# Weight chunks held behind the first row fetch, one branch moved, and stores and fetches of the expert stage reordered

## The chip, the cores and the metric

One of the eight cores of a Trainium2 chip runs the kernel. The metric is the device time of one execution in microseconds (us); the number given for the kernel before is the median of three runs. The profile is one further execution, and all positions in it are us from the start of its span.

## What is computed

The reference is one decoder layer on 576 tokens (512 of a prompt, 8 times 8 of samples) with a model width of 1024: a mixer of gated linear attention and dilated attention, a cross attention, a hierarchical mixture of experts, and a final normalisation. The change concerns the last two. Cut to what matters, that is:

```python
def hier_moe(x, w_gr, b_gr, w_er, b_er, w_e1, w_e3, w_e2):   # x: (576, 1024), normalised
    g_idx = jnp.argmax(x @ w_gr + b_gr, axis=-1)             # 4 groups, one for each token
    sel = (x @ w_er + b_er).reshape(N, 4, 8)[group g_idx]    # 8 experts in a group
    top_l, top_i = lax.top_k(sel, 2)                         # two experts for each token
    gate = p_group * softmax(top_l)
    y[token] = sum over its two experts e of
        gate * ((silu(x @ w_e1[e]) * (x @ w_e3[e])) @ w_e2[e])
h = h + hier_moe(rmsnorm(h, g3), ...)
y = rmsnorm(h, g_final)
```

Each of the 32 experts has 6 MB of float32 weights (two matrices of 1024 x 512 and one of 512 x 1024), so 192 MB are read whatever the tokens choose. Before this stage the kernel computes the mixer and the cross attention (some 580 us); the change does not touch them, apart from two memsets and from the weight loads that begin beside their end.

## The kernel before

**Tokens.** A route block computes group, experts and gates, and sorts the tokens: those of a group stand in 256 places, two tiles of 128 places each, tiles 2g and 2g+1. `pay` holds for each place the token's number (0 in an empty place) and its gates. The finished rows of the hidden state are written to a buffer in DRAM, `rows_d`, six 256 KB or smaller writes on GpSimd's queue and the last two on ScalarE's (L1111, L1120). GpSimd fetches a tile with an indirect DMA (`fetch_rows`, L1060) whose index `src` holds one row for each place, row 0 for an empty one. The first two tiles are fetched at the end of the route block (`i_first` is the second fetch), tiles 2 and 3 in the first pair, tiles 4 and 5 in pair 5 and tiles 6 and 7 in pair 9 (`fetch_group`, L1339), each into one of the four tiles `acc[:, t % 4]`. The same `acc` then collects the experts' output, so a tile can be fetched only after the finished rows of the tile that held its place before are stored.

**Pairs.** The loop at L1555 runs over 16 pairs of experts, p = 0 to 15; group g has pairs 4g to 4g+3. For each pair `slots_of` (L1476) builds four one-hot matrices `oh` on VectorE, `gather` (L1484) multiplies the group's rows with them on TensorE (32 matmuls at L1492) and brings the result into `X` (L1498 on ScalarE, L1500 on VectorE). The rows are split into two parts of float32 first, `pthi` on ScalarE and `ptlo` on VectorE (`split_group`, L1468, by lines L243 and L244), once for a group. Then come 64 matmuls with the weights w13 (L1566), the gated activation (L1588, L1591), four transposes (L1594), 32 matmuls with w2 (L1607), and `combine` (L1519), which adds the weighted result to `acc`. `scales` (L1502) prepares the weights of the places (L1510, L1513). The gather for the next pair is issued within the current one. After the last pair of a group `finish` (L1365) normalises its two tiles and stores them with two indirect DMAs on GpSimd's queue (`store_rows`, L1361); for the last group `last_norm` (L1534 to L1550) does this.

**Weights.** The 192 MB come as 12 chunks of 1 MB for each pair (8 of w13, 4 of w2; the last pair's w2 as 8 halves) into a ring of 18 buffers, issued by SyncE's queue (SP) in order (L1312, L1320, L1327), at most 8 in flight. A buffer is free again when the matmuls that read it are done. A manual dependency makes the chunk that is the sixteenth of the ring wait until `i_first` has landed:

```python
            if len(ring) == CHUNK_A + 3:
                tc.add_manual_dep(i_w.ins, i_first.ins.name, ..., reason="the first rows before more weights")
```

**Branch.** `general` (L1438) is a branch of the program that handles rare distributions of tokens; here it is not taken, and costs each engine the branch itself. It stands in pair p = GENERAL.

**Order.** A scheduler sets each engine's instruction order from the order of the code and the dependencies it finds; all engines then run their lists in order, with waits on semaphores between them. The names of lines in the rows are those of the kernel before.

Of the kernel before, what the change touches and what calls it, by code (L numbers as in the profile page):

```python
# [26 lines left out]
EPS = 1e-6  # L27
CHUNK_A, CHUNK_B = 13, 5
PAY = 24
GENERAL = 11  # L30
CUT = 128
KV = 4
OC = 2
# [142 lines left out]
def body(ctx: ExitStack, tc: tile.TileContext, I, O, dbg=None):  # L176
# [879 lines left out]
        ve.tensor_scalar(f[:, 0:1], id_, -1.0, 0.0, op0=OP.add, op1=OP.max)  # L1056
        ve.tensor_copy(out, f[:, 0:1])

    def fetch_rows(out, index):
        return gp.indirect_dma_start(out=out, out_offset=None, in_=rows_d[:, :],  # L1060
                                     in_offset=bass.IndirectOffsetOnAxis(ap=index, axis=0))

    def place_hot(out, at):

# [8 lines left out]
    def payload(ts, hots, bank):  # L1073

        for t, hot in zip(ts, hots):
            by_place(bank[:, (t - ts[0]) * 3 * PAY:(t - ts[0] + 1) * 3 * PAY], hot, pay3)
        n = len(ts) * PAY
        x = bank[:, 0:3 * n].rearrange("p (t s c) -> p t c s", s=3, c=PAY)
        ve.tensor_reduce(pay[:, ts[0]:ts[0] + len(ts)], x, axis=AX.X, op=OP.add)
        for t in ts:  # L1080
            row_index(dst[:, t:t + 1], pay[:, t], False)

    with ExitStack() as st:
        rp = pool(st, "route")
        space = acc.rearrange("p a c -> p (a c)")
        acc3, last = space[:, 0:T], space[:, T:2 * T]
        stage = [space[:, 2048 + i * 512:2560 + i * 512].rearrange("p (i c) -> p i c", c=128) for i in range(3)]
        stage4 = space[0:64, 3584:4096]
        hots = [space[:, a:a + 320].bitcast(BF16).rearrange("p (i c) -> p i c", c=128) for a in (2048, 3072)]
# [217 lines left out]
    def load_one(p, n):  # L1307

        w = wchunk()
        if n < 8:  # L1310
            q, h = divmod(n, 2)
            i_w = sy.dma_start(w, I["w13"][2 * p + h, q])  # L1312
            if len(ring) == CHUNK_A + 3:
                tc.add_manual_dep(i_w.ins, i_first.ins.name, mybir.DependencyInfo(
                    mybir.DependencyClass.Sync, mybir.DependencyReason.DATA), reason="the first rows before more weights")
            w = w.rearrange("p (k c) -> p k c", k=2)
            views[p, "in", q, h] = lambda k2, c: w[:, k2, c * 512:c * 512 + 512]
        elif p < 15:
            c, h = divmod(n - 8, 2)
            sy.dma_start(w, I["w2"][2 * p + h, c])  # L1320
            w = w.rearrange("p (j c) -> p j c", j=4)
            views[p, "out", c, h] = lambda j: w[:, j]
        else:
            c = n - 8
            w = w.rearrange("p (h j c) -> p h j c", h=2, j=4)
            for h in range(2):
                sy.dma_start(w[:, h], I["w2"][2 * p + h, c // 2].rearrange("p (j c) -> p j c", j=4)[  # L1327
                    :, :, c % 2 * 256:c % 2 * 256 + 256])
            views[p, "out", c, 0] = lambda j: w[:, 0, j]
            views[p, "out", c, 1] = lambda j: w[:, 1, j]  # L1330
# [8 lines left out]
    def fetch_group(g):  # L1339
        ts = [2 * g, 2 * g + 1]  # L1340
        for t in ts:
            read_index(src[:, t:t + 1], pay[:, t, 20:21])
            fetch_rows(acc[:, t % 4], src[:, t:t + 1])

    def payload_late(ts):
        bank = cp_()
        for i, t in enumerate(ts):
            hot = hot_()
            place_hot(hot, at8[:, :, t:t + 1])
            by_place(bank[:, i * 3 * PAY:(i + 1) * 3 * PAY], hot, pay3)  # L1350
        n = len(ts)
        ve.tensor_reduce(pay[:, ts[0]:ts[0] + n], bank[:, 0:3 * n * PAY].rearrange("p (t s c) -> p t c s", s=3, c=PAY),
                         axis=AX.X, op=OP.add)
        for t in ts:
            row_index(dst[:, t:t + 1], pay[:, t], False)

    loads_to(RING)
    gf = mw.tile([128, D], F32, name="gf")
    gp.dma_start(gf, I["g_fin"].to_broadcast([128, D]))

    def store_rows(x, index):  # L1361
        gp.indirect_dma_start(out=O["y"][:, :], out_offset=bass.IndirectOffsetOnAxis(ap=index, axis=0), in_=x, in_offset=None,
                              bounds_check=T - 1, oob_is_err=False)

    def finish(tiles):  # L1365

        n = len(tiles)
        s = mw.tile([128, 2, 2], F32, name="ss")
# [7 lines left out]
        ac.activation(r, r, AF.Exp, scale=-0.5)  # L1376
        for i, (a, index) in enumerate(tiles):
            ve.scalar_tensor_tensor(a, a, r[:, i:i + 1], gf, op0=OP.mult, op1=OP.mult)
            store_rows(a, index)


    def features(rows_, Xe):
# [151 lines left out]
    def last_norm(c, cs):  # L1534
# [8 lines left out]
        else:  # L1543
# [3 lines left out]
            gp.tensor_scalar(a[:, 0:CUT], a[:, 0:CUT], r, None, op0=OP.mult)  # L1547
            ac.activation(a[:, CUT:512], a[:, CUT:512], AF.Copy, scale=r)
            ve.scalar_tensor_tensor(a[:, 512:], a[:, 512:], r, gf[:, 512:D], op0=OP.mult, op1=OP.mult)
            store_rows(a, dst[:, 6 + c:7 + c])  # L1550

    split_group(0)
    oh, X = slots_of(0), tokens_x()
    so, done, nxt = None, None, None
    for p in range(16):  # L1555
        if p == 0:
            gather(0, oh, X, range(4))
        if p % 2 == 0 and p < 14 and p != GENERAL - 1:
            nxt = slots_of(p // 2 + 1), tokens_x()
        so = scales(p, oh)  # L1560
        H = [hp_(), hp_()]
# [7 lines left out]
        with tc.issue_after(i_h.ins):  # L1569
# [6 lines left out]
                payload_late([4, 5, 6, 7])  # L1576
            if p % 4 == 1 and 4 < p < 12:
                fetch_group(p // 4 + 1)
            if p % 4 == 2 and p < 14:
                split_group(p // 4 + 1)  # L1580
            if p == GENERAL:
                general()
                nxt = slots_of(p // 2 + 1), tokens_x()
                gather(p // 2 + 1, *nxt, range(4))
            elif nxt:
                gather(p // 2 + 1, *nxt, range(2) if p % 2 == 0 else range(2, 4))
        sg = mw.tile([128, 512], F32, name="sg")
        ac.activation(sg, H[0], AF.Silu, scale=sv[:, 0:1])  # L1588
        if p == 15:
# [23 lines left out]
                        combine(y, oT, p, z, last_norm)  # L1613
        if p % 4 == 0 and p:
            g = p // 4 - 1
            finish([(acc[:, t % 4], dst[:, t:t + 1]) for t in (2 * g, 2 * g + 1)])
        done = y, oT, p
        if p % 2 and nxt:
            (oh, X), nxt = nxt, None
# [15 lines left out]
```

## Time and profile before

| what | us |
|---|---|
| median of the three runs | 1088.97 |
| lowest and highest of them | 1088.72, 1091.85 |
| the profiled execution, its own time | 1092.6 |
| its span in the profile | 1090.9 |
| TensorE (PE) busy in the span | 1011.1 (93%) |
| VectorE (DVE), ScalarE (ACT), GpSimd (POOL) busy | 454.9, 342.2, 61.5 |
| mean granted TensorE clock, full speed is 1 | 0.961 |

The page gives, for 40 slices of the span, the busy share of each engine, the granted TensorE clock and what the DMA engines moved. The expert stage fills the slices from the 23rd on, where the DMA engines move 400 to 422 GB/s until the last slice; in the slices before, the rate lies between 29 and 350 GB/s. The clock is at 0.7 in four slices and at 0.8 to 0.9 or more in the others. A wait row names the waiting engine and line, then what ended the wait, then the total, the count and the longest wait, all in us.

### The profile page before, as it was taken

To read this page: it belongs to the slowest core of one execution; us is meant where nothing else is said; L and a number is where in the kernel's file an instruction comes from. 1 tells how busy PE (TensorE), PEld (TensorE's weight loads), DVE (VectorE), ACT (ScalarE), POOL (GpSimd) and SP (SyncE) were. 2 spreads that over 40 slices of the span, in tenths; PEclk is the share of its full clock that TensorE was granted. 3 is DMA by queue.
4 is the path that set the end of the run, shared out by engine and by line. 5 is a ranking of instruction groups with operands and counts; after the bars stand their busy time and mean duration, and the time that the engine had idled before them with its cause. 6 is when DMAs were issued, how large, how long until landed. Compare 5 with 4: busy or idle time off the path is not lost. (4 is left out here: it accounts for less than half of the span.)

```text
span 1090.9 us, 17977 instructions
## 1 busy us (share of the span) xinstructions
PE 1011.1 (93%) x7375; PEld 717.2 (66%) x7375; DVE 454.9 (42%) x1031; ACT 342.2 (31%) x696; POOL 61.5 (6%) x85
## 2 busy tenths in 40 slices
PE   8999999999999999999995699999599959799995
PEld 7998889886769999888995344445244434254432
DVE  6337775357555754554335224223222322113213
ACT  5355323367443533333322112113111311024103
POOL 2100011000000200000111000001000010001002
PEclk9999999999999999999997799999799979999998
DMA  7312115526785743564785499999999999999992
GB/s 254 118 39 78 29 57 232 208 72 225 313 314 175 263 172 123 204 209 180 271 350 198 176 417 422 420 421 422 421 421 420 421 420 422 419 420 421 420 402 100
DMA packets 59674, 301.91 MB, mean 277 GB/s; under 512 B 6935, under 2 KB 13576, under 8 KB 35136
## 3 DMA queue, kind: packets, MB, share of 16 engines
q1 hardware_dynamic: 53856, 282.66, 66.4%
q0 software_dynamic: 5120, 17.73, 4.4%
q8 instruction: 59, 0.97, 0.4%
q10 hardware_dynamic: 608, 0.30, 0.1%
q14 instruction: 31, 0.25, 0.1%
HBM read 290.30 MB, written 12.19 MB: 277 GB/s over the span
## 5 line engine op out<-in xcount | busy, mean ns | idle before, releaser
L1566 PE MATMUL hp<-wc,X 128*64 128x512 f32 x1024 | 229.4, 593 | 1.2 <-DMA wc<-w 1.2
L1566 PEld LDWEIGHTS hp<-wc,X 128*64 128x64 f32 x1024 | 89.1, 137 | 135.8 <-issue 127.5
L283 PE MATMUL pj<-hi,whi 128*128 128x288 f32 (+1 forms) x544 | 163.3, 301 | 0.9 <-ACT R1t L193 0.5
L283 PE MATMUL pj<-hi,wlo 128*128 128x288 f32 (+1 forms) x544 | 162.8, 299 | 0.0
L283 PE MATMUL pj<-lo,whi 128*128 128x288 f32 (+1 forms) x544 | 162.3, 299 | 0.0
L1607 PE MATMUL hp<-wc,sg 128*64 128x512 f32 (+1 forms) x544 | 121.4, 586 | 0.1
L234 ACT ACTIVATE whi<-wst 128x1024 fp32r<-128x1024 f32 (+1 forms) x62 | 65.6, 1058 | 148.0 <-PE pj L283 120.8
L283 PEld LDWEIGHTS pj<-hi,whi 128*128 128x128 f32 x544 | 103.4, 190 | 4.8 <-issue 2.6
L283 PEld LDWEIGHTS pj<-hi,wlo 128*128 128x128 f32 x544 | 103.7, 191 | 1.7 <-issue 1.4
L283 PEld LDWEIGHTS pj<-lo,whi 128*128 128x128 f32 x544 | 103.6, 190 | 1.3 <-issue 0.8
L235 DVE TENSOR_TENSOR wlo<-wst,whi 128x1024 fp32r<-128x1024 f32 (+1 forms) x62 | 76.0, 1226 | 44.8 <-ACT whi L234 44.8
L1607 PEld LDWEIGHTS hp<-wc,sg 128*64 128x64 f32 x544 | 39.2, 140 | 70.5 <-issue 66.7
L1591 DVE SCALAR_TENSOR_TENSOR sg<-hp,sv,sg 128x512 f32<-128x512 f32 x16 | 12.0, 749 | 162.8 <-PE hp L1566 154.7
L1588 ACT ACTIVATE sg<-hp,sv 128x512 f32<-128x512 f32 x16 | 11.0, 687 | 185.3 <-PE hp L1566 185.3
L1528 DVE TENSOR_TENSOR acc<-acc,cp 128x512 f32<-128x512 f32 (+1 forms) x66 | 42.3, 666 | 62.1 <-PE cp L1526 61.7
L244 DVE TENSOR_TENSOR ylo<-hp,yhi 128x512 fp32r<-128x512 f32 (+1 forms) x34 | 22.4, 659 | 78.5 <-ACT yhi L243 78.5
L308 PE MATMUL pj<-whi,hi 128*128 128x256 f32 (+1 forms) x184 | 52.9, 288 | 0.0
L308 PE MATMUL pj<-wlo,hi 128*128 128x256 f32 (+1 forms) x184 | 52.5, 286 | 0.0
L308 PE MATMUL pj<-whi,lo 128*128 128x256 f32 (+1 forms) x184 | 52.4, 285 | 0.0
L1492 PE MATMUL xp<-oh,pthi 128*128 128x256 f32 x128 | 35.5, 308 | 16.4 <-DVE oh L1480 9.2
L243 ACT ACTIVATE yhi<-hp 128x512 fp32r<-128x512 f32 (+1 forms) x34 | 19.4, 572 | 87.0 <-PE hp L1607 87.0
L1492 PEld LDWEIGHTS xp<-oh,pthi 128*128 128x128 f32 x128 | 27.3, 213 | 17.7 <-issue 16.9
(440 smaller groups left out, 1661.0 us busy)
## 6 DMA issues: line engine op xcount, KB each, us to landing
wc<-w SPq DMA_DIRECT2D x188, 1024.0 KB, 19.8
kv<-kc SPq DMA_DIRECT2D x16, 768.0 KB, 6.9
kv<-vc SPq DMA_DIRECT2D x16, 768.0 KB, 5.2
ckv<-mkc SPq DMA_DIRECT2D x16, 512.0 KB, 6.1
ckv<-mvc SPq DMA_DIRECT2D x16, 512.0 KB, 5.8
wst<-w_qkb SPq DMA_DIRECT2D x8, 512.0 KB, 3.7
wst<-w_mk SPq DMA_DIRECT2D x8, 512.0 KB, 5.5
wst<-w_mv SPq DMA_DIRECT2D x8, 512.0 KB, 4.5
```

Of the source, the lines that this page charges most:

```text
L234: ac.activation(hi[:, s], w[:, s], AF.Copy)
L235: ve.tensor_tensor(lo[:, s], w[:, s], hi[:, s].bitcast(F32), op=OP.subtract)
L243: ins = ac.activation(hi, x, AF.Copy)
L244: ve.tensor_tensor(lo, x, hi.bitcast(F32), op=OP.subtract)
L283: pe.matmul(p, lhsT=a[:, k], rhs=b[k][:, c], start=(k == 0 and s == 0), stop=(k == KT - 1 and s == 2))
L308: pe.matmul(outs[i][0:m], lhsT=a[xk][:, i * 128:i * 128 + m], rhs=b[:, k, :], start=(kh == 0 and k == 0 and s == 0 and head), stop=(kh == ...
L1492: pe.matmul(ps[:, k * 256:k * 256 + 256], lhsT=pt[s][:, c, kk * 128:kk * 128 + 128], rhs=oh[:, c], start=(k + c + s == 0), stop=(k + c + s ...
L1528: ve.tensor_tensor(a, a, ps, op=OP.add)
L1566: i_h = pe.matmul(H[c][rows[e]], lhsT=X[:, k, at + e * 64:at + e * 64 + 64], rhs=views[p, "in", k // 2, e](k % 2, c), start=(k == 0), stop ...
L1588: ac.activation(sg, H[0], AF.Silu, scale=sv[:, 0:1])
L1591: ve.scalar_tensor_tensor(sg, H[1], sv[:, 1:2], sg, op0=OP.mult, op1=OP.mult)
L1607: i_y = pe.matmul(Y[rows[e]], lhsT=hT_[:, j, rows[e]], rhs=views[p, "out", c, e](j), start=(j == 0), stop=(j == 3))
```

## The change

1. The manual dependency holds for the last three chunks of the ring (16th to 18th), where before it held for the 16th alone.
2. `slots_of(0)` is written ahead of `split_group(0)`, and the store index `dst` of the first two tiles is computed with those of tiles 2 and 3 later, in the first pair.
3. `GENERAL` is 9, where it was 11: the branch stands in the tenth pair. `split_group` of the next group is written in the pairs with p % 4 == 3, where it was p % 4 == 2; the next pair's slots are made, and gathered, to match.
4. The stores of finished rows are declared independent of one another.
5. Tiles 2 to 7 are fetched with an index that lies outside the buffer for an empty place, and such a place is left out by the DMA. `acc` is set to 0 once beforehand (two memsets on GpSimd, while the attention runs), since an empty place keeps what was there.

```diff
-GENERAL = 11
+GENERAL = 9
...
-    def fetch_rows(out, index):
+    def fetch_rows(out, index, some=False):
+        kw = dict(bounds_check=T - 1, oob_is_err=False) if some else {}
         return gp.indirect_dma_start(out=out, out_offset=None, in_=rows_d[:, :],
-                                     in_offset=bass.IndirectOffsetOnAxis(ap=index, axis=0))
+                                     in_offset=bass.IndirectOffsetOnAxis(ap=index, axis=0), **kw)
...
         ve.tensor_reduce(pay[:, ts[0]:ts[0] + len(ts)], x, axis=AX.X, op=OP.add)
-        for t in ts:
-            row_index(dst[:, t:t + 1], pay[:, t], False)
...
+        gp.memset(space[:, 2 * T:2048], 0.0)
+        gp.memset(space[64:128, 3584:4096], 0.0)
...
-            if len(ring) == CHUNK_A + 3:
+            if CHUNK_A + 2 < len(ring) <= RING:
...
-            read_index(src[:, t:t + 1], pay[:, t, 20:21])
-            fetch_rows(acc[:, t % 4], src[:, t:t + 1])
+            row_index(src[:, t:t + 1], pay[:, t], None)
+            fetch_rows(acc[:, t % 4], src[:, t:t + 1], True)
...
-        for t in ts:
+        for t in ts if ts[0] > 2 else [0, 1] + ts:
             row_index(dst[:, t:t + 1], pay[:, t], False)
...
+        if static:
+            for b in stored:
+                tc.declare_no_dep(i.ins, b, reason="other rows")
+            stored.append(i.ins)
...
+    oh, X = slots_of(0), tokens_x()
     split_group(0)
-    oh, X = slots_of(0), tokens_x()
...
-        if p % 2 == 0 and p < 14 and p != GENERAL - 1:
+        if p % 4 == 0 and p != GENERAL - 1 or p % 4 == 3 and p < 15:
             nxt = slots_of(p // 2 + 1), tokens_x()
...
-            if p % 4 == 2 and p < 14:
+            if p % 4 == 3 and p < 15:
                 split_group(p // 4 + 1)
...
             elif nxt:
-                gather(p // 2 + 1, *nxt, range(2) if p % 2 == 0 else range(2, 4))
+                gather(p // 2 + 1, *nxt, (range(2), range(2, 4), None, range(4))[p % 4])
```

On SyncE, where the ring is first filled, the last six loads stood like this before (the brackets hold the semaphores that a load waits for: HW ones belong to DMAs of SP and ACT, SW ones to DMAs of GpSimd; DMASW0 is here the first row fetches):

```order
L1312 DMA wc_6741<-w 128x2048 [waits DMAHW2_49]
L1312 DMA wc_6743<-w 128x2048 [waits DMAHW3_49,PE_49]
L1312 DMA wc_6745<-w 128x2048 [waits DMAHW6_49,PE_49]
L1312 DMA wc_6749<-w 128x2048 [waits DMAHW7_49]
L1312 DMA wc_6751<-w 128x2048 [waits DMAHW0_49,DVE_49]
L1312 DMA wc_6747<-w 128x2048 [waits DMAHW1_49,DMASW0_49]
```

With the change the same place reads (lines after the first insertion are a line or more further on):

```order
L1313 DMA wc_6731<-w 128x2048 [waits DMAHW2_49]
L1313 DMA wc_6733<-w 128x2048 [waits DMAHW3_49,PE_49]
L1313 DMA wc_6735<-w 128x2048 [waits DMAHW6_49,PE_49]
L1313 DMA wc_6737<-w 128x2048 [waits DMAHW7_49,DMASW0_49]
L1313 DMA wc_6739<-w 128x2048 [waits DMAHW0_49]
L1313 DMA wc_6741<-w 128x2048 [waits DMAHW1_49,DVE_49]
```

Before, one of the last five loads (the sixteenth chunk, wc_6747) stood behind the fetch and had been sorted to the end, so that four went ahead of it; now two go ahead and three stand behind.

On VectorE, between the first tiles' payload and the first gathered rows, the order before was:

```order
L1079 TENSOR_REDUCE pay<-sm 128x48
L244 TENSOR_TENSOR ptlo<-acc,pthi 128x2x256
L1043 TENSOR_SCALAR rowf<-pay 128x1 x2
L244 TENSOR_TENSOR ptlo<-acc,pthi 128x2x256
L1048 TENSOR_TENSOR rowf<-rowf,pay 128x1 x2
L244 TENSOR_TENSOR ptlo<-acc,pthi 128x2x256
L1049 SCALAR_TENSOR_TENSOR rowf<-rowf,pay 128x1 x2
L244 TENSOR_TENSOR ptlo<-acc,pthi 128x2x256
L1050 TENSOR_SCALAR rowf<-rowf 128x1 x2
L1480 TENSOR_TENSOR oh<-cs_61,pay 128x256
```

and is now:

```order
L1080 TENSOR_REDUCE pay<-sm 128x48
L244 TENSOR_TENSOR ptlo<-acc,pthi 128x2x256
L1489 TENSOR_TENSOR oh<-cs_61,pay 128x256 x2
L244 TENSOR_TENSOR ptlo<-acc,pthi 128x2x256 x3
L1509 TENSOR_SCALAR X<-xp,gmoe 128x256 x2
L1489 TENSOR_TENSOR oh<-cs_61,pay 128x256 x2
L1043 TENSOR_SCALAR rowf<-pay 128x1 x2
```

The first one-hot matrices stand behind one `ptlo` instead of four and six index operations, and the index operations behind the first `X`.

On ScalarE, the split for the third group (tiles 4 and 5, in pair 5) stands in the same place in both kernels; with the change it reads:

```order
L1597 ACTIVATE sg<-hp,sv 128x512
L243 ACTIVATE pthi<-acc 128x2x256
L1507 ACTIVATE X<-xp,gmoe 128x256 x2
L243 ACTIVATE pthi<-acc 128x2x256
L1607 ACTIVATE sg<-xp 128x512
L1523 ACTIVATE oT<-xp 128x256
```

and only the split for the last group, in pair 9, stands differently, behind the branch and two evacuations of `X`:

```order
L1449 UNCONDITIONAL_BRANCH x2
L1597 ACT_TABLE_LOAD
L1597 ACTIVATE sg<-hp,sv 128x512
L1507 ACTIVATE X<-xp,gmoe 128x256 x2
L243 ACTIVATE pthi<-acc 128x2x256
L1507 ACTIVATE X<-xp,gmoe 128x256 x2
```

So, although the code writes the split one pair later, the scheduler has left it where it was for the third group and moved it by a few instructions for the last.

## Rows read from the trace of the kernel before

**Rows 1.** Core by stretch: stretch, length, busy us (count) by engine, clock, DMA share, GB/s.

```profile
740.00:780.00 40.00, 28.80 (x144) 14.55 (x143) 11.02 (x21) 12.20 (x24) 4.76 (x4) 0.88 1.02 421
...
1020.00:1060.00 40.00, 39.43 (x174) 15.30 (x170) 5.62 (x10) 3.46 (x6) 0.00 (x0) 1.00 1.01 414
```

**Rows 2.** Waits of SP's queue from 500 us to the end.

```profile
SPq L1312 <- DMA wc<-w: 188.2, 91, 3.2
...
SPq L1312 <- PE hp L1566: 30.1, 17, 13.5
...
SPq L1312 <- DMA acc<-rows_d,src: 20.9, 1, 20.9
```

**Rows 3.** Waits of TensorE from 560 us to the end.

```profile
PE xp L1510 <- ACT X L1498: 23.7, 4, 11.5
PE xp L1492 <- DVE oh L1480: 9.2, 1, 9.2
PE xp L1492 <- DVEq L1440: 7.2, 1, 7.2
...
PE hp L1566 <- DMA wc<-w: 1.2, 2, 0.7
```

**Rows 4.** Two stretches of 4 us around the first gather, columns as in Rows 1.

```profile
612.00:616.00 4.00, 4.00 (x22) 3.05 (x21) 0.88 (x2) 1.68 (x4) 0.00 (x0) 0.79 0.01 4
...
620.00:624.00 4.00, 4.00 (x22) 1.41 (x20) 0.00 (x0) 0.00 (x0) 0.00 (x0) 1.00 0.88 320
```

**Rows 5.** DMA issues from 560 us: count, KB each, median us to landing.

```profile
rows_d<-acc POOLq DMA_DIRECT2D x3, 256.0 KB, 3.2
...
rows_d<-acc ACTq DMA_DIRECT2D x1, 256.0 KB, 9.8
```

**Rows 6.** DMA queues from 584 to 597 us: packets, MB, share (q1 SP, q10 ACT).

```profile
q1 hardware_dynamic: 472, 3.34, 66.9%
q10 hardware_dynamic: 608, 0.30, 7.6%
```

**Rows 7.** Timeline around the first fetch: start, us, engine, line, what [idle before].

```profile
585.90 0.70 ACTq L1120 DMA_DIRECT2D rows_d<-acc  x1
...
590.80 0.16 DVE L1204 CAST src<-rt 128x2 int32<-128x2 f32 x1
...
596.40 1.06 POOL L1060 DMA_INDIRECT acc<-rows_d,src  x1 [19.79 <-DVE rt L1271]
...
599.23 0.31 DVE L1079 TENSOR_REDUCE pay<-sm 128x48 f32<-128x144 f32 x1 [0.48 <-PE sm L1071]
...
604.23 2.19 ACT L243 ACTIVATE pthi<-acc 128x512 fp32r<-128x512 f32 x4 [9.83 <-DMA acc<-rows_d,src]
604.89 0.69 DVE L244 TENSOR_TENSOR ptlo<-acc,pthi 128x512 fp32r<-128x512 f32 x1 [5.36 <-ACT pthi L243]
...
607.83 0.41 DVE L1480 TENSOR_TENSOR oh<-cs,pay 128x256 fp32r<-128x256 f32 x1
...
608.39 0.55 PE L1492 MATMUL xp<-oh,pthi 128*128 128x256 f32 x1 [9.20 <-DVE oh L1480]
```

**Rows 8.** Timeline of GpSimd: a second store in pair 5, and the last two.

```profile
758.95 0.99 POOL L1362 DMA_INDIRECT o_y<-acc,dst  x1 [8.35 <-DMA o_y<-acc,dst]
...
1082.55 1.03 POOL L1362 DMA_INDIRECT o_y<-acc,dst  x1 [0.17 <-POOL acc L1547]
1086.82 0.97 POOL L1362 DMA_INDIRECT o_y<-acc,dst  x1 [3.25 <-DMA o_y<-acc,dst]
```

**Rows 9.** Timeline of TensorE right after its stall in pair 5.

```profile
779.31 7.01 PE L1607 MATMUL hp<-wc,sg 128*64 128x512 f32 x20
```

**Rows 10.** The chain that ended last, the weight chunk that ends the loads of w13.

```profile
1040.65 19.97 DMA wc<-w
```

**Rows 11.** GpSimd's DMA queue (q0) from 748 to 780 us, then from 995 to 1015 us.

```profile
q0 software_dynamic: 576, 1.71, 13.4%
...
q0 software_dynamic: 288, 0.49, 6.5%
```

More of the change, by code (lines that the diff above doesn't have):

```diff
@@ L1359, in body, with store_rows, finish @@
     gp.dma_start(gf, I["g_fin"].to_broadcast([128, D]))
[L1361 to L1365, printed above, removed]
+    stored = []
+    def store_rows(x, index, static=False):
+        i = gp.indirect_dma_start(out=O["y"][:, :], out_offset=bass.IndirectOffsetOnAxis(ap=index, axis=0), in_=x,
+                                  in_offset=None, bounds_check=T - 1, oob_is_err=False)
+        if static:
+            for b in stored:
+                tc.declare_no_dep(i.ins, b, reason="other rows")
+            stored.append(i.ins)
+    def finish(tiles, static=False):
         n = len(tiles)
@@ L1378, in finish @@
             ve.scalar_tensor_tensor(a, a, r[:, i:i + 1], gf, op0=OP.mult, op1=OP.mult)
-            store_rows(a, index)
+            store_rows(a, index, static)
     def features(rows_, Xe):
@@ L1549, in last_norm @@
             ve.scalar_tensor_tensor(a[:, 512:], a[:, 512:], r, gf[:, 512:D], op0=OP.mult, op1=OP.mult)
-            store_rows(a, dst[:, 6 + c:7 + c])
+            store_rows(a, dst[:, 6 + c:7 + c], True)
+    oh, X = slots_of(0), tokens_x()
     split_group(0)
-    oh, X = slots_of(0), tokens_x()
     so, done, nxt = None, None, None
@@ L1615, in body @@
             g = p // 4 - 1
-            finish([(acc[:, t % 4], dst[:, t:t + 1]) for t in (2 * g, 2 * g + 1)])
+            finish([(acc[:, t % 4], dst[:, t:t + 1]) for t in (2 * g, 2 * g + 1)], True)
         done = y, oT, p
```

## The prediction

> **What bounds the kernel now.** I read the core by stretch first, because shares of the whole span mix two regimes. From 620 us to the end of the weight loads the DMA engines are busy all the time: between 740 and 780 us the share is 1.02 at 421 GB/s although TensorE works only 28.80 of the 40 us, and between 1020 and 1060 us it is 1.01 with TensorE at 39.43 [rows 1]. A stall of TensorE in that stage therefore costs no transfer time; the ring of 18 chunks rides over it. The waits of SP say the same: the largest part is the wait for an earlier chunk to land (188.2 us), which is the limit of 8 in flight [rows 2]. The chain that ended last ends in weight transfers too: the last w13 chunk needs 19.97 us from its issue and lands at 1060.62 [rows 10]. What follows it is a fixed tail. But TensorE is close behind: in the whole stage it waited only 1.2 us for weights, while it lost 23.7 us to late `X`, 9.2 us to late one-hot matrices and 7.2 us to the branch [rows 3].
>
> So the end is set by three things: when the saturated stream begins, how many bytes it carries, and the tail. The stream begins late. Between 612 and 616 us the DMA share is 0.01; between 620 and 624 us it is 0.88 [rows 4]. In that hole the ring is full, and the next chunk waits up to 13.5 us for the first matmuls to free a buffer [rows 2]. They wait for the first gather at 608.39, this for one-hot matrices and split rows, these for the fetched rows, which release ScalarE at 604.23, and the fetch was issued only at 596.40 [rows 7].
>
> **The change part by part.** The sum is made against the profiled execution (1092.6, span 1090.9), which is 3.6 us above the median of the runs shown; I apply the difference to the median.
>
> *(a) Two chunks instead of four ahead of the row writes.* The index `src` of the first fetch is ready at 590.80 + 0.16 = 590.96, yet the fetch goes out at 596.40 [rows 7]. I take the other thing it waits for, the rows in DRAM, as the reason: the last write was issued at 585.90 [rows 7], and the 256 KB write on ScalarE's queue took 9.8 us, while writes of that size on GpSimd's queue, somewhat earlier, took 3.2 [rows 5]; 585.9 + 9.8 is 595.7, and GpSimd goes 0.7 us after that. With two chunks fewer in front, I expect the writes to land near 589 (585.9 + 3.2), before the index. The index then releases the fetch near 591.2: 596.40 - 591.2 = 5.2 us gained. Bounds: 0, if the writes stay at 9.8 us, and 5.4 (596.40 - 590.96). I take 5.2 because the two chunks left, 2.1 MB, are 5.0 us of transfer at 421 GB/s [rows 1], issued ahead of the writes. The three chunks held back cost nothing: pair 0 needs twelve, and they land in the hole.
>
> Between 584 and 597 us, 608 packets of the writes shared the engines with 472 of the weights, of some 7 KB each [rows 6]. The Trainium skill (DMA: Bandwidth & Descriptors, section Queues, rings and completion order) says that an engine with work on several queue rows takes a whole packet of each in turn. By that rule the 38 packets on each of 16 engines pay a weight packet each as long as any chunk is left; an estimate by it is that, with the second chunk in flight until 589, the writes land near 591.5, (a) is 1.5 us smaller, and the sum is -12.0 instead of -13.5.
>
> *(b) One-hot matrices ahead of most of the split.* From the fetched rows (604.23) to the first gather (608.39) are 4.16 us: one ACT split, then on DVE four `ptlo` with six index operations between them, then `oh` [rows 7]. Afterwards one `ptlo` stands ahead of `oh`. With the rows at 604.2 - 5.2 = 599.0, `pay` ends at 599.23 + 0.31 = 599.54, the `ptlo` at about 600.3, the first `oh` (0.41) at 600.7, the gather begins near 600.9. That is 7.5 earlier, 2.3 more than (a). Bounds: 0 if the gather now stalls on a later `ptlo`, and 2.8, the 607.83 - 604.89 between first `ptlo` and first `oh` without the 0.69 of one, plus what little follows. The remaining three `ptlo` (2.07) run beside the first half of the gather, and the deferred index operations beside pair 0: nothing is added on the path. Gather and first matmuls follow as before, so the stream begins 7.5 us earlier.
>
> *(c) Empty places are not fetched.* Two stores and two full fetches of group 0 and tiles 4, 5 moved 1.71 MB [rows 11]; 256 rows of 4096 B are 1.05 MB, so group 0 has 161 tokens and the other three 415 of their 768 places. 353 rows, 1.446 MB, leave the saturated stream; at 421 GB/s this is 3.4 us. An empty place still makes a packet: in the second stretch 288 packets with 120 rows (0.49 MB) took 6.5% of 20 us, 1.30 us, where the bytes alone need 1.16 [rows 11], so some 0.3 us is given back. I take 3.1; bounds 0 (skipping costs as much as fetching) and 3.5.
>
> *(d) Split, branch, store order within the stage.* In the order of instructions, the split for the third group has not moved, and its stall in pair 5 goes only as far as the fetch comes earlier: the second store waited 8.35 us for the first to land [rows 8], ahead of the fetches on POOL. I expect the two largest stalls of 11.5 us [rows 3] to shrink to below 5, and the branch's 7.2 us to move to pair 9. All of it lies beside saturated DMA: 0 in the sum. It matters as cover: TensorE is so near the bound that, if it shed nothing, (c) would be hidden behind it. What SP does at the branch holds its queue a few us with 8 chunks in flight, each landing 19.97 us after its issue [rows 10]: 0.
>
> *(e) The last two stores.* The second waited 3.25 us for the first to land and went out at 1086.82, against 1082.55 + 1.03 for the end of the first one's issue [rows 8]. Free, it goes at about 1083.9, so the end comes 2.9 us earlier; bounds 2.4 (two stores share the engines) and 3.25.
>
> The memsets stand on POOL while it is idle for tens of us: 0. Sum: -5.2 - 2.3 - 3.1 - 2.9 = **-13.5 us**: 1079.1 for the profiled execution, 1075.5 against the median.
>
> **The rivals.**
>
> *A. The first fetch is not held by the row writes,* or they are still slow. Then (a) is 0 and the rest stands: -8.3, 1080.7. For it: the profile names a DVE operation as what released the fetch [rows 7], and two chunks are still ahead. Against: that operation does not write the fetch's index, which had been done for 5.4 us. Chance 0.14.
>
> *B. TensorE becomes the bound,* since the split of the third group stays where it was. With stalls of 11 us left in pairs 5 and 9 and the branch beside them, TensorE gives no more than the 7.5 us of the start and the tail's 2.9, and (c) is lost: -10.4, 1078.6; the same time results if an empty place costs what a full one does. For it: 1.2 us of waiting for weights in 470 [rows 3]. Against: the two stores no longer wait for each other. Chance 0.13.
>
> *C. Slower: TensorE falls to its low clock where it starves.* Once the stalls are gone, TensorE is ahead of the weights and waits for each chunk in the last pairs. After the stall in pair 5 the mean clock of that stretch was 0.88 [rows 1], that is, it ran for a while at 1.2 GHz, and 20 matmuls took 7.01 us [rows 9], 0.35 each. A pair has 96, so 33.7 us, with the gathers more, against 12 x 2.49 = 29.9 us of transfer (1.05 MB at 421 GB/s). A pair wholly at the low clock loses 3.8 us; four such pairs eat the 13.5 us, seven (p = 9 to 15) give +13, 1102. It decides from four pairs on. Against: in the last pair TensorE already waited for chunks and the clock stayed at 1.00 [rows 1], and an engine that falls behind is busy again. The Trainium skill (TensorE: Matmul & The Clock Gate, section What's actually happening) says that half rate is the idle state; by that rule these pairs would come to 1102, and the 1.00 of the last pair does not agree with it. Chance 0.04.
>
> *D. The change does not do what it says,* in several parts at once: the fetch is not earlier, the gather stalls on the later `ptlo`, and skipped places cost as much as full ones; only the last store remains, -2.9, 1086.1. Chance 0.05.
>
> **How the numbers follow.** The forecast has 0.64, 1075.5. A measurement of this kernel can tell about 0.3% from no change, 3.3 us. Faster by more: forecast, A and B, 0.91; within: D, 0.05; slower: C, 0.04. All terms at their good ends give -15.0, 1074.0; (a) and (c) failing together, -5.2, 1083.8; all at their bad ends only the -2.4 of the tail, 1086.6. The runs shown lie within 3.1 us, so I put the range from 1074 - 3 = 1071 to 1085, which takes in A and B and leaves out C and D.
>
> **What would show it.** In the changed profile the 256 KB row write on ACT's queue should take 3 to 4 us to land, the first fetch should go out near 591, ScalarE's `pthi` begin near 599, the first gather near 601, and the stretch with DMA share near 0 end near 612 rather than 620. The last w13 chunk should land 10 to 11 us earlier, near 1050, and the last two stores stand 1.3 us apart. TensorE's wait for `X` should be under 10 us in total, and its wait for weights should rise from 1.2 us to 10 or more, at clock 1.00. The forecast is wrong in (a) if the fetch still goes near 596, in (c) if the time from the stream's start to that chunk is not 3 us shorter, and as a whole if the clock falls in pairs 12 to 15.

## The result, and the profile after

The changed kernel takes 1076.11 us (median of 4 runs, 1074.33 to 1076.97) against 1088.85 us for the kernel before (4 runs, 1086.38 to 1091.85). By these medians it is 12.7 us or 1.2% faster; the recorded ratio, which is not the quotient of the medians, is 0.9871, with a 95% interval of 0.9852 to 0.9889. Measured again beside the experiments (6 and 17 runs) it was 1079.43 against 1090.45, 11.0 us less, at a recorded ratio of 0.989 (0.9868 to 0.9912); the two intervals overlap. The profiled execution of the changed kernel took 1076.97, its span is 1075.3.

The spans differ by 15.6 us, more than the runs. The rest lies ahead of everything that the change touches: ScalarE issues the last row write at 585.90 in the kernel before [rows 7] and at 583.37 after. In a second profile of the same changed kernel that point lies at 587.31, and over the twelve profiles of this study, of kernels that differ little up to there, anywhere between 581.83 and 587.42, so these 2.5 us are not the change's. I count from that write from here on. The table takes the start of the first row fetch on GpSimd, the first gather on TensorE, the issue of the nineteenth weight chunk (the first that needs a buffer freed by TensorE; 619.38 and 609.08), the landing of the last w13 chunk (1060.62 and 1047.65) and the end of the span.

| stretch, us | before | after | difference | forecast |
|---|---|---|---|---|
| last row write to first fetch | 10.50 | 6.04 | -4.46 | -5.2 (a) |
| first fetch to first gather | 11.99 | 9.04 | -2.95 | -2.3 (b) |
| first gather to nineteenth chunk | 10.99 | 10.63 | -0.36 | 0 |
| nineteenth chunk to last w13 chunk | 441.24 | 438.57 | -2.67 | -3.1 (c) |
| last w13 chunk to the end | 30.28 | 27.65 | -2.63 | -2.9 (e) |
| sum | 505.00 | 491.93 | -13.07 | -13.5 |

The DMA issues of the changed kernel, from 560 us on (count, KB each, median us to landing), answer [rows 5]:

```profile
rows_d<-acc POOLq DMA_DIRECT2D x2, 256.0 KB, 2.8
...
rows_d<-acc ACTq DMA_DIRECT2D x1, 256.0 KB, 4.3
...
rows_d<-acc ACTq DMA_DIRECT2D x1, 32.0 KB, 4.0
```

The 256 KB row write on ScalarE's queue took 4.3 us where it had taken 9.8. The last write, issued at 583.37, is the 32 KB one; it took 4.0 us, and in the kernel before 9.5:

```profile
rows_d<-acc ACTq DMA_DIRECT2D x1, 32.0 KB, 9.5
```

The timeline of the changed kernel around the first fetch, as in [rows 7]:

```profile
583.37 0.50 ACTq L1121 DMA_DIRECT2D rows_d<-acc  x1
...
588.14 0.16 DVE L1205 CAST src<-rt 128x2 int32<-128x2 f32 x1
...
589.41 1.06 POOL L1061 DMA_INDIRECT acc<-rows_d,src  x1 [15.47 <-DVE rt L1169]
...
596.58 0.31 DVE L1080 TENSOR_REDUCE pay<-sm 128x48 f32<-128x144 f32 x1 [0.48 <-PE sm L1072]
596.61 2.19 ACT L243 ACTIVATE pthi<-acc 128x512 fp32r<-128x512 f32 x4 [4.86 <-DMA acc<-rows_d,src]
597.27 0.69 DVE L244 TENSOR_TENSOR ptlo<-acc,pthi 128x512 fp32r<-128x512 f32 x1 [0.38 <-ACT pthi L243]
597.88 0.76 DVE L1489 TENSOR_TENSOR oh<-cs,pay 128x256 fp32r<-128x256 f32 x2
598.41 0.29 PEld L1501 LDWEIGHTS xp<-oh,pthi 128*128 128x128 f32 x1 [2.02 <-ACT pthi L243]
598.45 0.55 PE L1501 MATMUL xp<-oh,pthi 128*128 128x256 f32 x1 [1.91 <-DVE oh L1489]
```

The writes now land near 587.4 (583.37 + 4.0), ahead of the index at 588.30, and the fetch leaves 1.1 us after the index. `oh` starts 0.61 us after the first `ptlo`, where 2.94 us lay between them before. TensorE's wait for `oh` is 1.9 us instead of 9.2.

TensorE's waits in the changed kernel, from 560 us on, answer [rows 3]:

```profile
PE xp L1501 <- DVEq L1449: 7.0, 1, 7.0
PE hp L1575 <- DMA wc<-w: 6.3, 9, 1.3
PE xp L1519 <- ACT X L1507: 6.0, 3, 4.7
...
PE xp L1501 <- DVE oh L1489: 1.9, 1, 1.9
```

The late `X` costs 6.0 us in place of 23.7, the branch as much as before, and TensorE now waits 6.3 us for weights in place of 1.2: at those moments it is ahead of the transfers. The stretches of the changed kernel that answer to [rows 4] and [rows 1] (columns as there):

```profile
604.00:608.00 4.00, 4.00 (x26) 2.33 (x26) 1.19 (x4) 1.22 (x3) 0.00 (x0) 1.00 0.43 176
608.00:612.00 4.00, 4.00 (x22) 1.42 (x20) 0.00 (x0) 0.00 (x0) 0.00 (x0) 1.00 0.46 133
612.00:616.00 4.00, 4.00 (x22) 1.31 (x20) 0.00 (x0) 0.00 (x0) 0.00 (x0) 1.00 1.00 422
```

```profile
740.00:780.00 40.00, 35.35 (x169) 16.49 (x167) 9.79 (x17) 7.23 (x13) 4.83 (x4) 0.96 1.01 420
...
860.00:900.00 40.00, 30.81 (x138) 15.22 (x135) 9.27 (x17) 7.79 (x14) 1.51 (x2) 0.91 1.01 418
...
980.00:1020.00 40.00, 37.06 (x161) 15.25 (x159) 5.71 (x11) 3.70 (x7) 0.00 (x0) 1.00 1.02 420
```

The DMA engines are saturated from 612 us on instead of some 620, and stay so. Between 980 and 1020 us TensorE lacks 2.9 of 40 us, waiting for chunks, and its clock is 1.00. The mean clock is lower where TensorE stood longer: 0.96 around the 4.7 us wait for `X` and 0.91 around the 7.0 us at the branch. The chain that ended last in the changed kernel is the same as before at its end, 13 us earlier:

```profile
1027.70 19.95 DMA wc<-w
1047.65 0.04 issue
1047.69 3.65 PE hp L1575 x12
```

Its last two stores on GpSimd follow each other at once, and so do those of the first group, where GpSimd stood idle for 8.35 us ahead of the second one before [rows 8]:

```profile
742.09 0.99 POOL L1367 DMA_INDIRECT o_y<-acc,dst  x1 [0.30 <-issue]
...
1069.59 1.04 POOL L1367 DMA_INDIRECT o_y<-acc,dst  x1 [0.17 <-POOL acc L1556]
1070.93 0.97 POOL L1367 DMA_INDIRECT o_y<-acc,dst  x1 [0.30 <-issue]
```

### The profile page after: what moved, and what is told of

The parts are those of the page before. It is cut to its first block, busy times and chain, and to the rows that moved or that the text cites. A ratio compares the mean times of both kernels' runs of the same rounds, so it can differ in the third digit from the quotient of the medians.

```text
span 1075.3 us, 17989 instructions
## 1 busy us (share of the span) xinstructions
PE 1019.0 (95%) x7375; PEld 711.8 (66%) x7375; DVE 456.6 (42%) x1043; ACT 340.6 (32%) x695; POOL 62.3 (6%) x87
## 5 line engine op out<-in xcount | busy, mean ns | idle before, releaser
L1575 PE MATMUL hp<-wc,X 128*64 128x512 f32 x1024 | 241.7, 595 | 6.3 <-DMA wc<-w 6.3
L283 PE MATMUL pj<-h1lo,whi 128*128 128x288 f32 x128 | 38.8, 303 | 0.0
```

Of the source, the lines that this page charges most:

```text
L283: pe.matmul(p, lhsT=a[:, k], rhs=b[k][:, c], start=(k == 0 and s == 0), stop=(k == KT - 1 and s == 2))
L1575: i_h = pe.matmul(H[c][rows[e]], lhsT=X[:, k, at + e * 64:at + e * 64 + 64], rhs=views[p, "in", k // 2, e](k % 2, c), start=(k == 0), stop ...
```

## The experiments

The theory is the forecast's: the end is the start of the saturated stream, plus the bytes in it, plus the tail, and the parts of the change add up. The rivals are that the first fetch was not held by the row writes, that TensorE bounds the stream, and that an empty place costs what a full one does. Five kernels undo one part each, one makes one part alone, two vary its size, one repeats the changed kernel, and one tries to go further. A run's median varies by some us from series to series, so times are given as ratios to the kernel before in the same series. The intervals of most ratios overlap, so causes are read from the stretches of the table above, from one profile of each kernel.

| kernel | ratio, 95% interval | write to fetch | write to gather | write to 19th chunk | to last w13 | to end |
|---|---|---|---|---|---|---|
| after, first profile | 0.9871 (0.9852, 0.9889) | 6.04 | 15.08 | 25.71 | 438.57 | 27.65 |
| after, again | 0.9890 (0.9868, 0.9912) | 6.17 | 15.32 | 25.55 | 438.27 | 27.57 |
| one chunk held, not three | 0.9923 (0.9903, 0.9944) | 9.64 | 19.25 | 30.45 | 438.31 | 27.61 |
| old order on VectorE | 0.9900 (0.9882, 0.9919) | 6.14 | 17.29 | 27.97 | 438.51 | 27.55 |
| full fetches | 0.9928 (0.9911, 0.9945) | 6.18 | 15.63 | 27.11 | 441.17 | 27.60 |
| dependent stores | 0.9913 (0.9893, 0.9933) | 6.18 | 15.65 | 26.51 | 438.52 | 30.35 |
| old split and branch | 0.9899 (0.9872, 0.9925) | 6.19 | 15.13 | 26.70 | 439.43 | 27.60 |
| before, three chunks held | 0.9969 (0.9953, 0.9985) | 5.96 | 17.30 | 28.09 | 441.73 | 30.35 |
| two chunks held | 0.9914 (0.9887, 0.9940) | 7.29 | 16.41 | 27.58 | 438.40 | 27.58 |
| five chunks held | 0.9905 (0.9878, 0.9932) | 6.18 | 16.02 | 26.46 | 439.00 | 27.56 |
| after, two edits more | 0.9881 (0.9858, 0.9904) | 6.01 | 14.97 | 25.63 | 438.39 | 26.91 |

### The changed kernel again

> The changed kernel once more, as the yardstick for the other kernels of this series. Ratio to before 0.987 as measured; the segments as in its first profile: fetch 6.0 us, first gather 15.1 us and nineteenth chunk 25.7 us after the issue of the last row write, 438.6 us from there to the last w13 chunk, 27.65 us to the end.

The stretches repeat within 0.3 us, while the ratio, expected at 0.987, came out at 0.989. The stretches are sharper than the times, and the differences below are taken against both profiles. They scatter unequally, though. In the seven profiles of kernels with skipped places, the new split and at most three chunks held, the stretch to the last w13 chunk lies between 438.27 and 438.57 us. The stretch to the nineteenth chunk varies by more than the 0.3 us, as the last section shows.

### One chunk held instead of three

```diff
-            if CHUNK_A + 2 < len(ring) <= RING:
+            if len(ring) == CHUNK_A + 3:
```

> The changed kernel with the manual dependency back on the sixteenth chunk alone (four chunks ahead of the row writes instead of two). If the fetch is held by the row writes, the 256 KB write on ACT's queue takes 9 to 10 us again (4.3 in the changed kernel), the first fetch goes out 10 to 11 us after the last row write's issue (6.0 there), and the kernel is 4 to 5 us slower than the changed one: 1080 to 1081, ratio to before about 0.992. If the fetch is held by VectorE instead, it stays at 6.0 us after that write's issue and the time stays at 1076.

The DMA issues of this kernel, and its first fetch on GpSimd:

```profile
rows_d<-acc ACTq DMA_DIRECT2D x1, 256.0 KB, 8.9
...
rows_d<-acc ACTq DMA_DIRECT2D x1, 32.0 KB, 8.6
```

```profile
591.47 1.06 POOL L1061 DMA_INDIRECT acc<-rows_d,src  x1 [18.93 <-PE sm L1184]
```

The larger write takes 8.9 us and the fetch leaves 9.64 us after the last write's issue (581.83), each a little less than expected, and the nineteenth chunk comes 4.7 to 4.9 us later than in the changed kernel. The small write landed 8.6 us after its issue, at 590.4, and the fetch starts 1.1 us after that. The row's bracket names a TensorE instruction (L1184) here and a VectorE one (L1169) in the changed kernel as what released the fetch. Neither writes the index or the rows, so the bracket is no proof of what the fetch waited for; the landing times and the changed dependency are.

### Three chunks held in the kernel before, nothing else

```diff
-            if len(ring) == CHUNK_A + 3:
+            if CHUNK_A + 2 < len(ring) <= RING:
```

> The kernel before with the manual dependency on three chunks and nothing else of the change. If the row writes hold the fetch, the 256 KB write lands in 4 to 5 us instead of 9.8, the fetch goes out 6.0 to 6.2 us after the last row write's issue instead of 10.5, the nineteenth chunk comes 4.5 to 5 us earlier (28.5 to 29 us after that write instead of 33.5), and the time falls by the same 4.5 to 5 us, ratio 0.9955. Rival A: the fetch stays at 10.5 us and nothing is gained.

The DMA issue of the write, and the first fetch on GpSimd:

```profile
rows_d<-acc ACTq DMA_DIRECT2D x1, 256.0 KB, 4.2
```

```profile
590.39 1.06 POOL L1060 DMA_INDIRECT acc<-rows_d,src  x1 [15.46 <-DVE rt L1168]
```

The write took 4.2 us (the landing of the smaller one is not in the trace), and the fetch left 5.96 us after the last write's issue, against 10.50. The nineteenth chunk came 5.4 us earlier, more than the 4.5 to 5 expected; the stretch from there to the last w13 chunk was 0.5 us longer, and the tail the same to 0.1 us. The time moved by a ratio of 0.9969 (0.9953 to 0.9985), 1.6 to 5.1 us. So the part works alone, in either kernel, and the rival that the fetch is held by something else has fallen.

### Two and five chunks held

```diff
-            if CHUNK_A + 2 < len(ring) <= RING:
+            if CHUNK_A + 3 < len(ring) <= RING:
```

> The changed kernel with two chunks held back instead of three, so three go ahead of the row writes. If the writes are slowed as long as weight packets stand beside them, the 256 KB write takes 5.5 to 7 us (4.3 with two ahead, 8.9 with four), lands after the index is ready, and the fetch goes out 7 to 8 us after the last row write's issue instead of 6.1; the kernel is 1 to 2 us slower than the changed one. If the slowing needs four chunks, the write stays at 4.3 us and nothing moves.

> The changed kernel with five chunks held back, none ahead of the row writes. The 256 KB write then takes 2.5 to 3.2 us, as on GpSimd's queue when it is quiet, but the fetch still goes out 6.0 to 6.2 us after the last row write's issue, because the index is ready no sooner: no gain at the start. The five chunks land one behind the other after the rows, so the nineteenth chunk lands later against its issue and the stretch to the last w13 chunk grows by 1 to 3 us: slower than the changed kernel by as much. If the writes still hold the fetch with two chunks ahead, the fetch comes earlier here and the kernel is faster than the changed one.

The second of these has `CHUNK_A < len(ring)`. The DMA issues of the two kernels, in this order (the landing of the 256 KB write is missing in the second):

```profile
rows_d<-acc ACTq DMA_DIRECT2D x1, 256.0 KB, 6.5
...
rows_d<-acc ACTq DMA_DIRECT2D x1, 32.0 KB, 6.2
```

```profile
rows_d<-acc ACTq DMA_DIRECT2D x1, 32.0 KB, 2.2
```

With none, two, three and four chunks ahead, the small write takes 2.2, 4.0, 6.2 and 8.6 us in these kernels, and the fetch leaves 6.18, 6.04 to 6.17, 7.29 and 9.64 us after it. Up to two chunks the index sets the fetch, beyond that the writes do. The landings in the traces say the same without any difference between kernels: the small write lands 0.6 to 1.3 us after the last of the chunks ahead of it in all ten profiles that show both, and in all eleven that show its landing the fetch starts 1.05 to 1.12 us after the later of that landing and the end of the index. With two chunks ahead the small write took between 3.5 and 4.9 us in the seven profiles that show it, and the index still came last. Holding five gains nothing at the start and costs 0.4 to 0.7 us between the nineteenth and the last w13 chunk, less than the 1 to 3 us expected: most of the five chunks are moved before the nineteenth is issued. Of the numbers tried, three held is the least that hides the writes.

### The old order on VectorE

```diff
+        for t in ts:
+            row_index(dst[:, t:t + 1], pay[:, t], False)
...
-        for t in ts if ts[0] > 2 else [0, 1] + ts:
+        for t in ts:
             row_index(dst[:, t:t + 1], pay[:, t], False)
...
+    split_group(0)
     oh, X = slots_of(0), tokens_x()
-    split_group(0)
```

> The changed kernel with the split ahead of the one-hot matrices again, and the ten index operations between them. If the order on VectorE sets the first gather, the time from the last row landing (ScalarE's first split) to the first gather rises from 1.8 to about 4.2 us, the stream begins 2 to 3 us later against the last row write, and the kernel takes 1078 to 1079. If the deferred work only moves the wait, for instance to the late second pair of one-hot matrices, the stream's start and the time stay at 1076.

Its first gather, on TensorE's timeline:

```profile
602.76 0.55 PE L1503 MATMUL xp<-oh,pthi 128*128 128x256 f32 x1 [4.02 <-DVE oh L1491]
```

From the first split on ScalarE (598.60) to this gather are 4.16 us, as in the kernel before; 1.84 in the changed one. The nineteenth chunk comes 2.3 to 2.4 us later. This is the forecast's term, 2.3. The run puts back the order of the split and the place of the index operations together; how the 2.3 us divide between them it does not show.

### Full fetches

```diff
-            row_index(src[:, t:t + 1], pay[:, t], None)
-            fetch_rows(acc[:, t % 4], src[:, t:t + 1], True)
+            read_index(src[:, t:t + 1], pay[:, t, 20:21])
+            fetch_rows(acc[:, t % 4], src[:, t:t + 1])
```

> The changed kernel with tiles 2 to 7 fetched in full, 353 rows or 1.446 MB more in the saturated stretch. If the bytes bound that stretch, the time from the nineteenth chunk's issue to the last w13 chunk's landing rises from 438.6 us by 2.7 to 3.4 us, and the kernel takes about 1079. If TensorE bounds it or a skipped place costs what a fetched one does, both stay within 0.7 us.

GpSimd's DMA queue in the changed kernel between 739 and 775 us (two stores, two fetches), then in this one between 735 and 790:

```profile
q0 software_dynamic: 576, 1.15, 8.3%
```

```profile
q0 software_dynamic: 576, 1.71, 7.8%
```

The packets are as many, the bytes 0.56 MB less with skipping, which are the 136 empty places of tiles 4 and 5 with 4096 B each. The stretch to the last w13 chunk grows by 2.6 to 2.9 us, back to the 441.2 of the kernel before. Neither rival holds: an empty place costs far less than a full one, and most of the time of the bytes is gained. The nineteenth chunk also came 1.4 to 1.6 us later in this profile, for which the edit gives no reason; the last section of this document comes back to it. The ratio lies 0.0038 to 0.0057 above the changed kernel's, 4 to 6 us, more than the 3 expected, and these 1.4 to 1.6 us are part of that.

### Dependent stores

```diff
-            for b in stored:
-                tc.declare_no_dep(i.ins, b, reason="other rows")
```

> The changed kernel without the declaration that stores are independent, so each second store waits for the first again. My theory: the tail from the last w13 chunk to the end rises from 27.65 to about 30.3 us, that is +2.6, and TensorE's stall in pair 5 returns to about 11 us without any further cost: about 1078.7. Rival B, TensorE as the bound: the returned stalls in pairs 5 and 9 cost several us on top, in the time from the nineteenth chunk to the last w13 chunk, 1082 or more.

The waits of TensorE and then the last stores in this kernel:

```profile
PE xp L1517 <- ACT X L1505: 11.4, 3, 10.3
...
PE hp L1573 <- DMA wc<-w: 3.2, 6, 0.7
```

```profile
1074.37 1.04 POOL L1367 DMA_INDIRECT o_y<-acc,dst  x1 [0.17 <-POOL acc L1554]
1078.66 0.97 POOL L1367 DMA_INDIRECT o_y<-acc,dst  x1 [3.25 <-DMA o_y<-acc,dst]
```

The stall in pair 5 is back at 10.3 us, where the changed kernel has 4.7, TensorE's wait for weights falls from 6.3 to 3.2 us, and the stretch to the last w13 chunk stays at 438.52 us. The tail is 30.35 us, 2.7 to 2.8 more. A stall that is 5.6 us longer thus cost nothing, and what this part gains from the nineteenth chunk on lies in the last two stores. (The nineteenth chunk came 0.8 to 1.0 us later in this profile; the edit touches nothing that stands before it.)

### The old split and branch

```diff
-GENERAL = 9
+GENERAL = 11
...
-            if p % 4 == 3 and p < 15:
+            if p % 4 == 2 and p < 14:
                 split_group(p // 4 + 1)
```

with the conditions of the slots and of the gather as in the kernel before.

> The changed kernel with the branch back in the twelfth pair and the split written a pair earlier. My theory: TensorE's waits move about (the stall before pair 9's matmuls returns to several us, the branch's 7 us go to pair 11), all beside saturated DMA, so the 438.6 us from the nineteenth chunk to the last w13 chunk and the time stay the same within 0.7 us. Rival B, TensorE as the bound: that stretch grows by 2 us or more, 1078 or above.

The stretch to the last w13 chunk is 439.43 us, 0.9 to 1.2 more than in the changed kernel, above the 0.7 that I had allowed and below the 2 of the rival. The DMA engines were busy from 980 to 1044 us (share 1.00 to 1.03 in every 4 us of it, although two chunks, at 993.87 and 1032.15, landed 3.4 us after those before them in place of 2.5), so there it was not TensorE that held them. Whether the part is worth 1 us or nothing this run does not settle: 439.43 lies outside the 438.27 to 438.57 of the seven profiles above, but the ratios, 0.9899 and 0.9890, have intervals that overlap almost wholly, and with full fetches the stretch took 441.24 and 441.73 us with the old split (the kernel before and the one with three chunks held) against 441.17 with the new one. That TensorE's stalls bound the stream is excluded by the stores' kernel.

### Two edits more

```diff
-    gp.dma_start(gf, I["g_fin"].to_broadcast([128, D]))
+    i_gf = gp.dma_start(gf, I["g_fin"].to_broadcast([128, D]))
+    tc.add_manual_dep(i_gf.ins, i_first.ins.name, ..., reason="the first rows first")
...
-            gp.tensor_scalar(a[:, 0:CUT], a[:, 0:CUT], r, None, op0=OP.mult)
-            ac.activation(a[:, CUT:512], a[:, CUT:512], AF.Copy, scale=r)
+            ac.activation(a[:, 0:512], a[:, 0:512], AF.Copy, scale=r)
```

> The changed kernel with two more edits: the load of the final gain (512 KB) waits for the first rows, and the last normalisation leaves no multiplication on GpSimd, ScalarE taking its columns. If the gain's load slows the second fetch, the rows land about 1 us earlier (12 us after the last row write's issue instead of 13.1), but the first gather only 0.3 to 0.4 us earlier, since the payload is ready no sooner. In the tail the first store no longer stands behind two multiplications on GpSimd: the end comes 1.2 us earlier, 26.4 us after the last w13 chunk. Together 1.5 us faster than the changed kernel, about 1074.5; against: a store that waits for ScalarE gains nothing if ScalarE's longer operation is late.

The tail of this kernel on GpSimd:

```profile
1071.31 1.05 POOL L1369 DMA_INDIRECT o_y<-acc,dst  x1 [4.85 <-ACT tail_s L1557]
1072.67 0.96 POOL L1369 DMA_INDIRECT o_y<-acc,dst  x1 [0.30 <-issue]
```

The first edit missed: the rows land 12.97 us after the last write's issue, against 13.08 and 13.32, so the load of the final gain was not what slowed the second fetch. The second edit shortens the tail by 0.7 us of the 1.2 expected: ScalarE is done with the first tile at 1070.60, but GpSimd starts its store 0.7 us later, where in the changed kernel it waited 0.17 us behind its own multiplication. The time, 0.9881 (0.9858 to 0.9904), cannot be told from the changed kernel's.

## Why the prediction was right

The time came out at 1076.11 where 1075.5 was forecast, and the parts as well as the sum are in the traces. That the sum of the stretches came within 0.4 us of the forecast is in part luck: (a) fell short by 0.7 us, and two gains that were not forecast made up for it, 0.6 us of rows that landed sooner after their fetch and 0.4 us between the first gather and the nineteenth chunk.

(a) The mechanism is shown: the row writes held the fetch, and they are slow because weight chunks stand beside them (9.8 us with four in the kernel before, 4.2 there with two). The term was too large by 0.7 us: I let the fetch leave 0.24 us after the index, and it leaves 1.1 us after it (588.30 to 589.41). The trace of the kernel before already shows this: the 9.8 us belong to the 256 KB write, issued at 585.40; the write issued at 585.90 is the 32 KB one, it landed after 9.5 us at 595.4, and GpSimd followed 1.0 us later, not 0.7. The 3.2 us on GpSimd's queue are also the median of the last three 256 KB writes there; over all seven it is 7.5.

The estimate from the Trainium skill (DMA: Bandwidth & Descriptors, section Queues, rings and completion order), 1.5 us less than my term, was too low by 0.8: the writes landed near 587.4, 4.0 us after their issue, not after 5.6. (With the forecast's own 0.7 us behind a landing at 591.5 it would have been 1.0 less.) The third and the fourth chunk add 2.2 and 2.4 us to the small write, nearly the 2.5 us of transfer that a chunk is: the write is slowed for as long as chunks are in flight, which agrees with the rule. That alone could also be a plain queue, but the packets show turns. These are the DMA queues of the kernel before from 590 to 592 us (q1 carries the weights, q10 the row writes):

```profile
q1 hardware_dynamic: 94, 0.70, 91.6%
q10 hardware_dynamic: 95, 0.05, 8.0%
```

The engines took as many packets of the one queue as of the other. Turns are not the whole of it: before 589 us, more than 3 us after the first issue, no packet of the writes had gone, for which no run shows the reason, and 352 of the 608 went from 592 to 594 us, as the weights ran out.

(b) `oh` ahead of most of the split was worth 2.3 us when undone, 2.95 between the two first profiles. From the first split on ScalarE to the gather the two differ by 2.32 us (4.16 and 1.84). The other 0.63 are the rows, which landed sooner after their fetch (7.20 us from the start of the fetch to that split, 7.83 before), for which the change gives no reason. (Eight index operations, not six, stood ahead of the first `oh` in the kernel before; the sum did not use their number.) The gather did not stall on the later `ptlo`.

(c) 2.67 us came instead of 3.1; by the undone part 2.6 to 2.9. Of 3.4 us for the bytes, some 0.7 are given back for 353 empty places, more than the 0.3 that I had read from the stores' queue [rows 11]; with a scatter of 0.3 us in that stretch the difference is small.

(d) The stalls shrank as forecast (23.7 to 6.0 us for `X`, the largest 4.7, the branch as before) and turned in part into waiting for weights: 6.3 us, where 10 or more were forecast. The stall that the stores cause costs nothing; whether split and branch bring up to 1 us is open. What I had called cover is there: with the stall put back, TensorE still waited 3.2 us for weights.

(e) 2.63 us came instead of 2.9; undone 2.7 to 2.8.

The rivals: A fell with the kernel that has the first part alone, B with the dependent stores and the full fetches. C did not happen: there were 9 waits for weights, the longest 1.3 us, four of them between 980 and 1020 us, and the clock stayed at 1.00 in that stretch. The Trainium skill's half rate for an idle engine (TensorE: Matmul & The Clock Gate, section What's actually happening) thus does not bear on gaps of this kind here; and the 1.00 of the last pair in the kernel before, with waits of 0.7 us at most, was no evidence against it. C's price was also too low. Its 20 matmuls [rows 9], from 779.31 to 786.32, span a rise of the clock, as these stretches of the kernel before show:

```profile
780.00:784.00 4.00, 4.00 (x12) 1.18 (x10) 2.05 (x4) 0.83 (x2) 0.00 (x0) 0.50 1.00 412
784.00:788.00 4.00, 4.00 (x20) 1.25 (x18) 0.69 (x1) 0.60 (x1) 0.00 (x0) 0.95 1.00 418
```

Wholly at 1.2 GHz ten of them took 4.22 us (from a start at 780.22 to one at 784.44), 0.42 each and not 0.35; 96 are 40.5 us, a pair would have lost some 11 us and not 3.8, and two such pairs, not four, would have cost more than the whole gain. D fell with A and B. What I had not foreseen is the spread of the runs, some 3 us between series, as large as any single part of the change but (a), and the two unforecast gains above.

## What to carry to other kernels

Where a kernel streams weights at the full rate, split the time into the start of the stream, its bytes and its tail; here the parts of the change in different stretches added up, and stalls of up to 10.3 us of the engines beside the stream cost nothing that could be shown. A stall long enough to empty the ring was not tried. A small transfer on the critical path was slowed by large ones that happened to be in flight, so hold back those that have time, and only until something else (here the index) sets the start. The releaser that a profile names for a transfer with many waits can be an innocent one; set the landing times beside the start, change the suspected transfer and look.

## What was not expected of the hardware

How fast a gather turns into a free buffer depends on when TensorE's clock rises. From the first gather to the nineteenth chunk the kernels, whose instructions there are nearly the same, took 10.2 to 11.6 us. Core by stretch, the changed kernel, whose gather began at 598.45, and then the one with the old split and branch, whose gather began at 601.20:

```profile
600.00:602.00 2.00, 2.00 (x11) 1.90 (x9) 1.70 (x5) 0.00 (x0) 0.00 (x0) 0.50 1.03 430
602.00:604.00 2.00, 2.00 (x10) 1.06 (x9) 1.19 (x11) 0.84 (x2) 0.00 (x0) 0.93 0.98 414
```

```profile
604.00:606.00 2.00, 2.00 (x7) 0.95 (x6) 1.94 (x13) 0.84 (x2) 0.00 (x0) 0.50 1.00 422
606.00:608.00 2.00, 2.00 (x11) 1.21 (x10) 0.00 (x0) 0.00 (x0) 0.00 (x0) 0.76 1.02 430
```

The first is at 2.4 GHz from a little after 602 on, some 4 us after its gather began; the second still ran at 1.2 GHz until nearly 607, some 6 us after. Their stretches to the nineteenth chunk are 10.63 and 11.57 us. The full fetches, whose gather began at 600.15, and the second profile of the changed kernel, whose gather began at 602.63, fit in:

```profile
604.00:606.00 2.00, 2.00 (x4) 0.39 (x5) 0.89 (x10) 0.78 (x2) 0.00 (x0) 0.57 1.02 430
```

```profile
604.00:606.00 2.00, 2.00 (x13) 1.86 (x11) 1.70 (x5) 0.00 (x0) 0.00 (x0) 0.64 1.01 422
```

By these means the clock rose near 605.7, 5.6 us after the gather's start, and near 605.4, 2.8 us after it; the stretches are 11.48 and 10.23 us. A rise that comes 1.7 to 1.9 us later costs 0.9 us, as half the rate for that long would. So 0.9 of the 1.4 us by which the nineteenth chunk came later with full fetches than in the changed kernel's first profile is the clock. Why the clock rose sooner or later no run shows.

GpSimd took 1.0 to 1.1 us from the last thing it waited for to the start of the first fetch, whether that was the index on VectorE (588.30 to 589.41) or the landing of a write. It took 0.9 us from the landing of a store: in the kernel with dependent stores, the first of the last two lands at 1077.76, and the second starts at 1078.66. Behind ScalarE it took 0.7 us (1070.60 to 1071.31, the last kernel above), and behind its own multiplication 0.17.
